# Group softmax, streamed through four buffers: smaller first and last tiles, and a drain behind each of the last waits on GpSimd

## The chip, the cores and the metric

The kernel runs on one core of a Trainium2 chip. The metric is the device time of one execution in microseconds. The kernel before was run four times: 1327.36, 1332.95, 1336.01 and 1332.74 us, median 1332.84 us. One further execution was profiled; it took 1332.72 us, and its recorded span is 1330.2 us.

## The reference

The input is a float32 tensor of 4 x 4096 x 4352. Each row of 4352 numbers is cut into 8 groups of 544, and each group gets its own softmax.

```
x_g = x.reshape(B, N, G, Dg)                      # G = 8, Dg = 544
x_g = x_g - x_g.max(axis=-1, keepdims=True)
exp = np.exp(x_g)
out = exp / exp.sum(axis=-1, keepdims=True)
return out.reshape(B, N, D).astype(np.float32)
```

Input and output are 285 MB each. There are 131,072 groups; spread over 128 partitions that is 1024 groups per partition.

## The kernel before

**Tiles.** A tile of size s holds s groups in each of the 128 partitions, so 128 x s x 544 numbers. The list `sizes` gives the tiles in order: one of 16 groups, 41 of 24 (`T`), one of 16 and one of 8; `nt` is 44 and the sum is 1024. Tile t lives in buffer t modulo 4 (`NT = 4`, each buffer as large as a tile of 24).

**Work on a tile.** ScalarE takes the exponential in place, in parts of at most 12 groups (`C`, function `parts`; line L92). The maximum is not subtracted. VectorE adds up each part (L102), takes the reciprocal of all the sums of the tile (L106), multiplies the tile by them in place (L109) and keeps a running maximum of the sums and their reciprocals (L114). At the very end `judge` tests that maximum (L119 to L134); were the test to fail, a slower and safer loop would redo everything. With this input it isn't entered.

**Queues.** SyncE's queue (SP) issues all loads in order (L139). The load of tile t waits until the store of tile t - 4 has landed, because it takes over its buffer. GpSimd's queue (POOL) issues the stores in order (L146), each when VectorE has counted the tile as scaled. The last two tiles (`LAST = 2`) are stored by SP instead (L142), behind the last load. After its last store POOL waits for the last two of its own stores (L148), drains (L149), and then waits for the two stores that SP issued; that ends the program's work.

**Loops.** ScalarE and VectorE run tile 0 by itself, then a loop of 10 turns of 4 tiles (`turns`, `looped`), then the remaining three tiles. In the loop all tiles have 24 groups. Semaphores are set back by fixed amounts after tile 0 and after each turn. The order on each engine is the order of the program text; no scheduler moves anything.

Of the kernel before, what the change touches and what calls it, by code (L numbers as in the profile page):

```python
# [9 lines left out]
def kernel(  # L10
# [5 lines left out]
    nc = tc.nc  # L16
    G = 8
    P = 128
    NT = 4
    LAST = 2  # L20
    C = 12
    LOW, HIGH = 1e-6, 1e30
    f32 = mybir.dt.float32
    X = mybir.AxisListType.X
# [6 lines left out]
    Dg = D // G  # L31
    per = N * G // P
    T = 3 * G
    sizes = [16] + [T] * (per // T - 1) + [16, 8]
    assert sum(sizes) == per
    nt = len(sizes)
    turns = (nt - 1 - LAST) // NT
    start = [sum(sizes[:t]) for t in range(nt + 1)]
    xg_all = xf.rearrange("n (g d) -> (n g) d", d=Dg)
    og_all = of.rearrange("n (g d) -> (n g) d", d=Dg)  # L40
# [5 lines left out]
    def dram(a, t):  # L46
        lo, hi = start[t] * P, start[t + 1] * P
        return a[lo:hi, :].rearrange("(p g) d -> p (g d)", p=P)

    def parts(t):  # L50
        return [(c, min(c + C, sizes[t])) for c in range(0, sizes[t], C)]

    before = [0]
    for t in range(nt):
        before.append(before[-1] + len(parts(t)))

    landed = [tc.alloc_semaphore(f"landed{b}") for b in range(NT)]
    stored = [tc.alloc_semaphore(f"stored{b}") for b in range(NT)]
    last_stored = tc.alloc_semaphore("last_stored")
    exp_done = tc.alloc_semaphore("exp_done")  # L60
    sum_done = tc.alloc_semaphore("sum_done")
    rec_done = tc.alloc_semaphore("rec_done")
    scaled = tc.alloc_semaphore("scaled")
    kept = tc.alloc_semaphore("kept")
# [18 lines left out]
    def groups(b, lo, hi):  # L83
        return bufs[b][:, lo * Dg:hi * Dg].rearrange("p (g d) -> p g d", d=Dg)

    def buf(t):
        return bufs[t % NT][:, :sizes[t] * Dg]

    def scalar_tile(t, landed_at):
        b = t % NT  # L90
        for k, (lo, hi) in enumerate(parts(t)):
            i = nc.scalar.activation(  # L92
                out=groups(b, lo, hi), in_=groups(b, lo, hi), func=Exp, scale=1.0)
            if k == 0:
                i.wait_op(landed[b], landed_at, "sem-ge")
            i.then_inc(exp_done, 1)

    def vector_tile(t, exp_at, at):
        b = t % NT
        size = sizes[t]  # L100
        for k, (lo, hi) in enumerate(parts(t)):
            i = nc.vector.reduce_sum(  # L102
                out=vals[:, b, 0, lo:hi], in_=groups(b, lo, hi), axis=X).wait_op(
                exp_done, exp_at + k + 1, "sem-ge")
        i.then_inc(sum_done, 1)
        nc.vector.reciprocal(out=vals[:, b, 1, :size], in_=vals[:, b, 0, :size]).wait_op(  # L106
            sum_done, at + 1, "sem-ge").then_inc(rec_done, 1)
        xg = groups(b, 0, size)
        nc.vector.tensor_tensor(  # L109
            out=xg, in0=xg,  # L110
            in1=vals[:, b, 1, :size].unsqueeze(2).to_broadcast([P, size, Dg]),
            op=op.mult,
        ).wait_op(rec_done, at + 1, "sem-ge").then_inc(scaled, 1)
        nc.vector.tensor_tensor(  # L114
            out=peak[:, :, :size], in0=peak[:, :, :size], in1=vals[:, b, :, :size], op=op.max,
        ).wait_op(kept, at + 1, "sem-ge").then_inc(kept, 1)
# [27 lines left out]
    for t in range(nt - LAST):  # L144
        nc.gpsimd.wait_ge(scaled, t + 1)
        nc.gpsimd.dma_start(out=dram(og_all, t), in_=buf(t)).then_inc(stored[t % NT], 16)  # L146
    for t in range(nt - NT, nt - LAST):
        nc.gpsimd.wait_ge(stored[t % NT], 16 * (t // NT + 1))  # L148
    nc.gpsimd.drain()  # L149
    nc.gpsimd.wait_ge(last_stored, 16 * LAST)  # L150

    looped = range(1, 1 + NT)
    rest = range(1 + turns * NT, nt)
    turn = before[1 + NT] - before[1]

    nc.scalar.preload_act_table(Exp)  # L156
    scalar_tile(0, 16)
    nc.scalar.sem_inc(landed[0], -16)
    with nc.scalar.Fori(0, turns):
        for t in looped:  # L160
            scalar_tile(t, 16)
# [2 lines left out]
        scalar_tile(t, 16)  # L164

    nc.vector.memset(peak[:, :, :], 0.0).then_inc(kept, 1)  # L166
    vector_tile(0, 0, 0)
    for s, n in ((exp_done, before[1]), (sum_done, 1), (rec_done, 1), (kept, 1)):
        nc.vector.sem_inc(s, -n)
    with nc.vector.Fori(0, turns):  # L170
        for k, t in enumerate(looped):
            vector_tile(t, before[t] - before[1], k)
        for s, n in ((exp_done, turn), (sum_done, NT), (rec_done, NT), (kept, NT)):
            nc.vector.sem_inc(s, -n)
    for k, t in enumerate(rest):
# [72 lines left out]
```

## Time and profile before

| what | value |
|---|---|
| median of 4 runs | 1332.84 us |
| the profiled execution, its own time | 1332.72 us |
| its span | 1330.2 us |
| VectorE busy | 1195.1 us (90%) |
| ScalarE busy | 478.4 us (36%) |
| moved by DMA | 570.45 MB, mean 429 GB/s |
| loads of 24 groups, issue to landing | 38.6 us (median of 41) |
| stores of 24 groups by GpSimd | 51.2 us (median of 41) |

The span is what the recorder covers; the 2.5 us between it and the execution's own time lie around it. "DMA share" in a table of stretches is the mean busy share of the core's 16 DMA engines; a packet is booked where it starts, so that the share of a single microsecond swings and can exceed 1. One packet here is the part of a tile that belongs to one partition, so a larger tile has longer packets.

### The profile page before, as it was taken

Reading aid. Unit: us, or ns where it says so; the run is one execution under the profiler, and the core shown is the slowest. Engines: PE = TensorE matmul, PEld = TensorE weight load, DVE = VectorE, ACT = ScalarE, POOL = GpSimd, SP = SyncE. Lnnn points to the kernel's source line nnn. Section 1 sums busy time; section 2 is a strip of 40 time slices with the busy share of each in tenths; the row PEclk is TensorE's granted clock in tenths of the full one; section 3 lists DMA queues with packets and bytes.
Section 4 is the critical chain, followed back from the end, with each engine's and each line's share of the span. In section 5 each row is a group of like instructions: output and inputs, shape, how many; then the busy total and the mean of one; then the engine's idle time right before and its main releaser. Section 6 shows DMA issues by size and latency. Waiting matters only on the chain.

```text
span 1330.2 us, 604 instructions
## 1 busy us (share of the span) xinstructions
PE 0.2 (0%) x2; PEld 0.1 (0%) x2; DVE 1195.1 (90%) x226; ACT 478.4 (36%) x88; POOL 22.7 (2%) x46
## 2 busy tenths in 40 slices
PE   0000000000000000000000000000000000000000
PEld 0000000000000000000000000000000000000000
DVE  4999999889998999999998899999999989888996
ACT  3533333344333333333344443333333333433321
POOL 0000000000000000000000000000000000000000
DMA  9999999999999999999999999999999999999997
GB/s 410 417 444 427 427 438 432 432 430 440 432 430 433 441 427 433 440 432 429 433 441 430 433 430 443 427 430 440 437 427 430 441 430 429 429 446 427 431 415 307
DMA packets 12674, 570.45 MB, mean 429 GB/s; under 512 B 1408, under 2 KB 1408, under 8 KB 1408
## 3 DMA queue, kind: packets, MB, share of 16 engines
q1 hardware_dynamic: 6624, 291.90, 50.9%
q0 software_dynamic: 6048, 278.53, 48.4%
q14 instruction: 2, 0.02, 0.0%
HBM read 285.21 MB, written 285.21 MB: 429 GB/s over the span
## 4 chain that ended last, share of the span: by engine, by line
another core or an unknown queue 71%; DVE 17%; DMA 8%; issue 2%; ACT 1%; SPq 1%; DVEq 0%; PE 0%; POOLq 0%
DVE vals L102 9%; DVE xt L109 7%; DMA xt<-in_x_dram 4%; DMA out_dram<-xt 4%; ACT xt L92 1%; SPq L139 1%; DVE vals L106 0%; DVE peak L114 0%; DVE within L124 0%; DVE extreme L120 0%; PE found L128 0%; DVE count L132 0%; DVEq L170 0%; DVE verdict L134 0%
## 5 line engine op out<-in xcount | busy, mean ns | idle before, releaser
L92 ACT ACTIVATE xt<-xt 128x6528 f32<-128x6528 f32 (+1 forms) x87 | 477.2, 5531 | 826.2 <-DMA xt<-in_x_dram 826.2
L102 DVE TENSOR_REDUCE vals<-xt 128x12 f32<-128x6528 f32 (+1 forms) x87 | 589.5, 6817 | 118.5 <-ACT xt L92 118.5
L109 DVE TENSOR_TENSOR xt<-xt,vals 128x13056 f32<-128x13056 f32 (+2 forms) x44 | 587.2, 13346 | 1.5
L146 POOL DMA_DIRECT2D out_dram<-xt x42 | 22.5, 536 | 1266.2 <-DVE xt L109 1266.2
L106 DVE RECIPROCAL vals<-vals 128x24 f32<-128x24 f32 (+2 forms) x44 | 13.1, 298 | 1.5
L114 DVE TENSOR_TENSOR peak<-peak,vals 128x48 f32<-128x48 f32 (+2 forms) x44 | 8.8, 200 | 0.0
L156 ACT ACT_TABLE_LOAD x1 | 1.3, 1283 | 0.9 <-PEq L232 0.9
L166 DVE MEMSET peak<- 128x48 f32 x1 | 0.1, 98 | 1.1 <-PEq L232 1.1
L132 DVE TENSOR_REDUCE count<-found 1x1 f32<-1x2 f32 x1 | 0.1, 149 | 0.3 <-PE found L128 0.3
L128 PE MATMUL found<-within,one 128*1 128x2 f32 x2 | 0.2, 164 | 1317.5 <-DVE within L124 1317.5
L124 DVE TENSOR_SCALAR within<-extreme 128x1 f32<-128x1 f32 x2 | 0.2, 148 | 0.0
L120 DVE TENSOR_REDUCE extreme<-peak 128x2 f32<-128x48 f32 x1 | 0.2, 203 | 0.0
L134 DVE CAST verdict<-count 1x1 int32<-1x1 f32 x1 | 0.1, 142 | 0.0
L128 PEld LDWEIGHTS found<-within,one 128*1 128x1 f32 x2 | 0.1, 80 | 1317.5 <-DVE within L124 1317.5
L232 POOL MEMSET const-float32-0.0<- 128x1 f32 x1 | 0.1, 99 | 0.3 <-issue 0.3
L232 POOL MEMSET const-bfloat16-1.0<- 128x1 bf16 x1 | 0.1, 102 | 0.0
L232 POOL MEMSET const-uint8-127<- 128x1 uint8 x1 | 0.1, 100 | 0.0
L232 POOL MEMSET const-float32-1.0<- 128x1 f32 x1 | 0.1, 99 | 0.0
L119 DVE MEMSET one<- 128x1 f32 x1 | 0.1, 59 | 0.0
## 6 DMA issues: line engine op xcount, KB each, us to landing
xt<-in_x_dram SPq DMA_DIRECT2D x41, 6528.0 KB, 38.6
out_dram<-xt POOLq DMA_DIRECT2D x41, 6528.0 KB, 51.2
xt<-in_x_dram SPq DMA_DIRECT2D x2, 4352.0 KB, 23.6
out_dram<-xt POOLq DMA_DIRECT2D x1, 4352.0 KB, 30.5
out_dram<-xt SPq DMA_DIRECT2D x1, 4352.0 KB, 16.3
xt<-in_x_dram SPq DMA_DIRECT2D x1, 2176.0 KB, 27.4
out_dram<-xt SPq DMA_DIRECT2D x1, 2176.0 KB, 11.8
```

Of the source, the lines that this page charges most:

```text
L92: i = nc.scalar.activation(out=groups(b, lo, hi), in_=groups(b, lo, hi), func=Exp, scale=1.0)
L102: i = nc.vector.reduce_sum(out=vals[:, b, 0, lo:hi], in_=groups(b, lo, hi), axis=X).wait_op(exp_done, exp_at + k + 1, "sem-ge")
L106: nc.vector.reciprocal(out=vals[:, b, 1, :size], in_=vals[:, b, 0, :size]).wait_op(sum_done, at + 1, "sem-ge").then_inc(rec_done, 1)
L109: nc.vector.tensor_tensor(out=xg, in0=xg, in1=vals[:, b, 1, :size].unsqueeze(2).to_broadcast([P, size, Dg]), op=op.mult,).wait_op(rec_done ...
L114: nc.vector.tensor_tensor(out=peak[:, :, :size], in0=peak[:, :, :size], in1=vals[:, b, :, :size], op=op.max,).wait_op(kept, at + 1, "sem-g ...
L120: nc.vector.reduce_max(out=extreme[:, :], in_=peak[:, :, :], axis=X).wait_op(kept, at + 1, "sem-ge").then_inc(tested, 1)
L124: nc.vector.tensor_scalar(out=within[:, k:k + 1], in0=extreme[:, k:k + 1], scalar1=most, scalar2=None, op0=op.is_le).then_inc(tested, 1)
L128: nc.tensor.matmul(out=found[:, :], lhsT=one[:, :], rhs=within[:, :], start=True, stop=True).then_inc(counted, 1)
L139: nc.sync.dma_start(out=buf(t), in_=dram(xg_all, t)).then_inc(landed[t % NT], 16)
L146: nc.gpsimd.dma_start(out=dram(og_all, t), in_=buf(t)).then_inc(stored[t % NT], 16)
L156: nc.scalar.preload_act_table(Exp)
L232: nc = _bacc.Bacc("TRN2", target_bir_lowering=False, num_devices=1)
```

## The change

The first tiles become 8, 12 and 12 groups in place of 16, and the last ones 16, 12 and 4 in place of 16 and 8; there are 40 tiles of 24 instead of 41, and 46 tiles in all instead of 44. Tiles that are not of 24 groups are worked on in parts of at most 8 groups (`FINE`) instead of 12. The first three tiles run ahead of the loop, whose turns remain 10. `LAST` stays 2, so SP stores the tiles of 12 and 4, and GpSimd stores the tile of 16. At the end GpSimd waits for its last eight stores, not its last two, and it drains after each of these eight waits, not once after all.

```
+    FINE = 8
+    HEAD = 3
+    TAIL = 3
...
-    sizes = [16] + [T] * (per // T - 1) + [16, 8]
+    sizes = [8, 12, 12] + [T] * (per // T - 2) + [16, 12, 4]
...
-    turns = (nt - 1 - LAST) // NT
+    turns = (nt - HEAD - TAIL) // NT
...
     def parts(t):
-        return [(c, min(c + C, sizes[t])) for c in range(0, sizes[t], C)]
+        size = C if sizes[t] == T else FINE
+        return [(c, min(c + size, sizes[t])) for c in range(0, sizes[t], size)]
...
-    for t in range(nt - NT, nt - LAST):
+    for t in range(nt - LAST - 8, nt - LAST):
         nc.gpsimd.wait_ge(stored[t % NT], 16 * (t // NT + 1))
-    nc.gpsimd.drain()
+        nc.gpsimd.drain()
     nc.gpsimd.wait_ge(last_stored, 16 * LAST)
...
-    looped = range(1, 1 + NT)
-    rest = range(1 + turns * NT, nt)
-    turn = before[1 + NT] - before[1]
+    looped = range(HEAD, HEAD + NT)
+    rest = range(HEAD + turns * NT, nt)
+    turn = before[HEAD + NT] - before[HEAD]
...
-    scalar_tile(0, 16)
-    nc.scalar.sem_inc(landed[0], -16)
+    for t in range(HEAD):
+        scalar_tile(t, 16)
+        nc.scalar.sem_inc(landed[t % NT], -16)
...
-    vector_tile(0, 0, 0)
-    for s, n in ((exp_done, before[1]), (sum_done, 1), (rec_done, 1), (kept, 1)):
+    for t in range(HEAD):
+        vector_tile(t, before[t], t)
+    for s, n in ((exp_done, before[HEAD]), (sum_done, HEAD), (rec_done, HEAD), (kept, HEAD)):
         nc.vector.sem_inc(s, -n)
```

More of the change, by code (lines that the diff above doesn't have):

```diff
@@ L171 @@
         for k, t in enumerate(looped):
-            vector_tile(t, before[t] - before[1], k)
+            vector_tile(t, before[t] - before[HEAD], k)
         for s, n in ((exp_done, turn), (sum_done, NT), (rec_done, NT), (kept, NT)):
```

## The prediction, made before the changed kernel was run

> **What bounds the kernel now.** I first read the page, then its DMA part against the engines' busy times.
>
> ```profile
> span 1330.2 us, 604 instructions
> ...
> PE 0.2 (0%) x2; PEld 0.1 (0%) x2; DVE 1195.1 (90%) x226; ACT 478.4 (36%) x88; POOL 22.7 (2%) x46
> ...
> DMA packets 12674, 570.45 MB, mean 429 GB/s; under 512 B 1408, under 2 KB 1408, under 8 KB 1408
> ...
> q1 hardware_dynamic: 6624, 291.90, 50.9%
> q0 software_dynamic: 6048, 278.53, 48.4%
> ```
>
> The two queues' packets fill 99.3% of the 16 DMA engines' span; VectorE, the next, has 90%. Where the missing part lies, a table of stretches shows (columns: stretch and length, then busy time of PE, PEld, DVE, ACT and POOL, clock, DMA share, GB/s).
>
> ```profile
> 0.00:2.00 2.00, 0.00 (x0) 0.00 (x0) 0.10 (x1) 1.08 (x1) 0.20 (x4) 1.00 0.35 87
> 2.00:34.00 32.00, 0.00 (x0) 0.00 (x0) 14.29 (x4) 12.34 (x4) 0.00 (x0) 1.00 0.99 421
> 240.00:1240.00 1000.00, 0.00 (x0) 0.00 (x0) 902.35 (x162) 358.96 (x65) 17.06 (x32) 1.00 1.00 433
> 1290.00:1305.00 15.00, 0.00 (x0) 0.00 (x0) 14.93 (x4) 3.27 (x1) 0.00 (x0) 1.00 0.91 392
> 1305.00:1308.00 3.00, 0.00 (x0) 0.00 (x0) 3.00 (x3) 0.56 (x1) 0.00 (x0) 1.00 0.08 35
> 1308.00:1324.00 16.00, 0.19 (x2) 0.09 (x2) 9.63 (x10) 0.00 (x0) 0.00 (x0) 1.00 0.98 418
> 1324.00:1328.00 4.00, 0.00 (x0) 0.00 (x0) 0.00 (x0) 0.00 (x0) 0.00 (x0) 1.00 0.07 28
> ```
>
> At 433 GB/s the bytes need 1317.4 us, so 12.8 us of span are not full transfer. The stretches shown account for 12.0 of them: 1.3 us at the start, 0.3 to 34, 1.4 in 1290 to 1305, 2.8 in the hole from 1305 to 1308, 0.3 to 1324, 3.7 to 1328, 2.2 after it. Now the point on which I decide: in the hole the share is 0.08 and in 1324 to 1328 it is 0.07, close to one engine of 16 (0.0625). I read this as one slow engine, about 4.5 us behind the other 15, which works through the hole on its backlog and sets the last landing at 1328.7. Fifteen engines waste the hole; the one that ends the program doesn't.
>
> The tail of the timeline, the issues and the drain (a row of GpSimd's queue that the page doesn't count as busy):
>
> ```profile
> 1288.42 9.27 DVE L102 TENSOR_REDUCE vals<-xt 128x12 f32<-128x6528 f32 x2
> 1298.01 9.22 DVE L109 TENSOR_TENSOR xt<-xt,vals 128x8704 f32<-128x8704 f32 x1
> 1307.27 10.01 SPq L142 DMA_DIRECT2D out_dram<-xt  x2
> 1312.21 4.69 DVE L109 TENSOR_TENSOR xt<-xt,vals 128x4352 f32<-128x4352 f32 x1
> ```
> ```profile
> xt<-in_x_dram SPq DMA_DIRECT2D x1, 2176.0 KB, 27.4
> out_dram<-xt SPq DMA_DIRECT2D x1, 4352.0 KB, 16.3
> out_dram<-xt SPq DMA_DIRECT2D x1, 2176.0 KB, 11.8
> ```
> ```profile
> L149 POOLq DRAIN  x1: 3496/3496/3496, 1314.6 to 1314.6; - x1
> ```
>
> The last store is issued at 1316.9 and lands 11.8 us later though its bytes need 5.1 us.
>
> **The change part by part.** A group costs 0.643 us each way (278.5 kB at 433 GB/s), 1.287 us both ways.
>
> *Head.* Before, the first four loads hold 88 groups, 56.6 us of transfer. After, they hold 56, 36.0 us, until about 38. Is a store there by then? The first load landed 13.0 us after issue; 8 groups fewer take 5.1 off, so it lands at 8.8. ScalarE 3.8 (the 8-group form), VectorE 4.7 + 0.2 + 4.7, with gaps and 0.3 on POOL: the first store goes out at about 22.7 instead of 38.8. Tile 1 takes VectorE 4.7 + 2.4 + 0.2 + 6.9 + 0.2 (half the 13.76 us multiply of 24 groups), so its store goes out near 37; tile 2's near 51.5. Load 4 waits for store 0. While store 0 is on its way the engines have it to move, and all that is queued, loads 36.0 and store 0 5.1, ends at about 43; store 1 has then been waiting since 37 and covers load 4's issue. If store 0 took the 30.5 us that the first one took before, it would land at 53; work of loads, store 0 and store 1 lasts to 51 and store 2 goes out at 51.5, a hole of 2 us at most. I take 0, by the share of 0.99 to 1.00 near it; ends 0 and +2. VectorE begins 5.1 us earlier, which is worth nothing while DMA is full.
>
> *Two more tiles,* so four more DMAs. All 88 of them together cannot have cost the slow engine more than its 4.5 us of lag, 0.05 each: 0 to +0.2 us, I take 0.1. The Trainium skill, "DMA: Bandwidth & Descriptors", section on the anatomy of one DMA, speaks against the change here: about 2.0 us fixed per DMA beside its bytes. Four of these on the path would make, as an estimate, 8 us and about 1340.7 us; this trace, full at 433 GB/s through 1000 us, shows that cost covered by other queued transfers.
>
> *Middle.* Tiles of 24, loop and their waits are as before: 0. The smaller parts (at most 8 groups) touch head and tail alone; ScalarE has 64% of its time free, and VectorE pays 0.1 us for 2 x 4.68 instead of 9.27 on the tile of 16.
>
> *Tail.* The last tile of 24 was there at 1254.8 with 24 groups behind it; now 32 are behind it, 8 x 1.287 = 10.3 us earlier: 1244.5. Then ScalarE's first part 5.65, VectorE 28.0 (1260.44 to 1288.42 now) to 1278.1, the 16 groups 18.9 to 1297.0, the 12 groups 14.5 (4.68 + 2.41 + 0.2 + 6.9 + 0.2, gaps) to 1311.5, the 4 groups 5.1 (2.41 + 0.2 + 2.35 + gaps) to 1316.6. So the last tile is scaled as late as before (1316.9), but what then is left is smaller: 2.6 us of bytes instead of 5.1. The slow engine needs it by 1328.4 - 2.6 - 1.0 for issue = 1324.8: 8.2 us of slack, and it never runs dry. The loads may run up to 7.7 us later against the stores than they do now (the last load of 24 landed 7.7 us after the issue of the next, 1247.0). And the last load may be as slow as the 27.4 us row: that one was issued at 1274.3 with 72 groups of stores and 8 of loads behind it, this one will have 56 and 4, 20 x 0.643 us fewer, so it is issued at 1287.2, lands at 1314.6 and is scaled, after ScalarE's 2.0 and VectorE's 5.1, at 1321.7. Each alone still makes the 1324.8. Gain: 0, because the bytes of the slow engine are the same. Ends: 0, and +4 if both delays add up.
>
> *Waits and drains.* Behind them on POOL stands only the wait for SP's stores; nobody waits for POOL until the end. One drain is 3.5 us (L149), others of POOL at the program's end 0.03 to 0.11. The store of 16 groups goes out at 1297.3; eight drains of 3.5 are 28 us, to 1325.3. The last also follows that store's landing: by the last store of POOL before (25.9 us) at 1323.2, plus 3.5 = 1326.7, under the 1328.7 of SP's last store. By the 30.5 us row it would be 1331.3. I take 0, two microseconds from being exposed; ends 0 and +2.6.
>
> *Sum.* 1330.2 + 0 + 0.1 + 0 + 0 = 1330.3 of span, and 2.5 around it: 1332.8; the profiled execution stands 0.1 us under the median of the runs. With the drain so close I say 1333.0.
>
> **Rivals.** *Faster:* the chain of waits names ScalarE and VectorE in the tail, and if these and not the slow engine set the end, the first landing is 5.1 us earlier and the last store 2.6 us shorter: 1332.7 - 7.7 = 1325.0. For it speaks the hole at 1305. Against it: the engine at work in the hole, and a DMA share of 1.00 that cannot pass on an early start.
>
> *Slower:* drains that cannot start while a store of POOL is under way. Then all eight follow the landing at 1323.2, 28 us to 1351.2, 22.5 later than now: 1355. It decides from eight drains longer than 0.7 us each on. For it: the one drain took 3.5 us with nothing left in its queue, thirty times the others. Against it: the others show that a drain with no work is short.
>
> *A late tail:* the last load lands after about 1318 and the slow engine runs dry: +4, 1337.
>
> *No change:* that is my forecast.
>
> **How the numbers follow.** No change 0.62; faster 0.15; serial drains 0.13; late tail 0.10. About 0.5% (6.7 us) can be told from no change by a measurement of this kernel. Half the late tail lies beyond it with the spread of the runs, and a little of the forecast on the fast side: faster 0.17, same 0.63, slower 0.20. The forecast's own range is the spread of the runs, 1328 to 1338. For 8 in 10 it takes in the faster case (1325) and the late tail with that spread (1341), not the serial drains.
>
> **What would show it.** Right: full DMA share from 34 to 1290, first store near 22.7, the last VectorE multiply ending near 1316, one engine alone in the last 4 us, the last drain ended before the last landing. Wrong: a share under 0.9 between 38 and 55; a hole after the last load without one busy engine; a drain as the last thing before the end; or a last landing several microseconds before 1328, which would show that the slow engine was no floor.

## The result, and the profile after

The changed kernel is slower by a third of a per cent: the ratio of its time to that of before is 1.0034, with a 95% interval of 1.0022 to 1.0045, which is 4.5 us of 1327.6 (2.9 to 6.0). The medians are 1334.06 us (52 runs, 1326.63 to 1339.07) and 1327.62 us (78 runs of the kernel before, 1324.52 to 1337.06). Single executions of either kernel spread over 12 us, and unevenly: 40 of the 78 of before lie under 1328 us, 2 of the 52 of the change. So the medians are 6.4 us apart, the means (1333.84 and 1329.36) 4.5 us, as the ratio says. The profiled execution of the changed kernel took 1335.07 us with a span of 1333.2 us, against 1332.72 and 1330.2 of the one profile of before that the prediction had. That one profile was of an execution 5.1 us above the median that 78 runs gave later. So the two profiles differ by 3.0 us in span, less than the kernels do, and the place where time went is read from the stretches, not from that difference.

The middle is as forecast. From the page of the changed kernel, its head line and its DMA issues (size, then median time from issue to landing), and one row of its timeline (start, duration, engine, line):

```profile
span 1333.2 us, 628 instructions
...
xt<-in_x_dram SPq DMA_DIRECT2D x40, 6528.0 KB, 46.9
out_dram<-xt POOLq DMA_DIRECT2D x40, 6528.0 KB, 42.9
```
```profile
23.66 0.67 POOL L150 DMA_DIRECT2D out_dram<-xt  x1 [23.20 <-DVE xt L113]
```

The first store goes out at 23.7 instead of 38.8 us. But look at the two medians. Before, a load of 24 groups took 38.6 us from issue to landing and a store 51.2; now they take 46.9 and 42.9. The sum is the same (89.8 us both times). By the median the loads of the long middle have become 8.3 us slower and the stores 8.3 us faster, though no tile there differs. Below I call the *gap* the time by which a load lands after the next load has been issued. A tile's transfers come every 30.9 us, so the gap is the load's time less 30.9: 7.7 us before, 16.0 now.

Next the stretches of the changed kernel (columns as in the prediction: stretch, length, busy PE, PEld, DVE, ACT, POOL, clock, DMA share, GB/s), and the tail of its timeline:

```profile
240.00:1240.00 1000.00, 0.00 (x0) 0.00 (x0) 903.14 (x162) 357.64 (x64) 17.00 (x32) 1.00 1.00 433
1240.00:1281.00 41.00, 0.00 (x0) 0.00 (x0) 37.95 (x8) 14.85 (x3) 0.53 (x1) 1.00 0.98 422
1281.00:1287.00 6.00, 0.00 (x0) 0.00 (x0) 6.00 (x3) 3.88 (x2) 0.53 (x1) 1.00 0.53 226
1287.00:1316.00 29.00, 0.00 (x0) 0.00 (x0) 28.86 (x9) 7.22 (x3) 0.53 (x1) 1.00 0.96 401
1316.00:1319.00 3.00, 0.00 (x0) 0.00 (x0) 3.00 (x3) 0.53 (x1) 0.00 (x0) 1.00 0.14 58
1319.00:1330.00 11.00, 0.19 (x2) 0.09 (x2) 5.17 (x10) 0.00 (x0) 0.00 (x0) 1.00 0.96 407
1330.00:1332.00 2.00, 0.00 (x0) 0.00 (x0) 0.00 (x0) 0.00 (x0) 0.00 (x0) 1.00 0.02 9
```
```profile
1251.60 11.18 ACT L96 ACTIVATE xt<-xt 128x6528 f32<-128x6528 f32 x2 [19.80 <-DMA xt<-in_x_dram]
...
1285.51 0.53 POOL L150 DMA_DIRECT2D out_dram<-xt  x1 [30.44 <-DVE xt L113]
...
1304.36 0.53 POOL L150 DMA_DIRECT2D out_dram<-xt  x1 [18.32 <-DVE xt L113]
...
1318.37 5.44 SPq L146 DMA_DIRECT2D out_dram<-xt  x2
...
1321.02 2.42 DVE L113 TENSOR_TENSOR xt<-xt,vals 128x2176 f32<-128x2176 f32 x1
```

There are two holes in the DMA share: 6 us at 0.53, which end when VectorE has finished the last tile of 24 and POOL issues its store (1285.5), and 3 us at 0.14, which end when SP issues the store of the tile of 12 (1318.4). In both VectorE is busy without a break. And the last tile of 24 was there at 1251.6, not at 1244.5. At the end no single engine is left over: the share goes from 0.96 to 0.02, and by the trace's landing records the 16 engines finish within 1.2 us of each other (1330.0 to 1331.2). In the profile of before, one engine landed 3.3 us after the other 15.

The landing records show one thing more. Each transfer lands in 16 parts, one from each engine. In this execution of the changed kernel the parts of one load of 24 lie within 2.4 us at 76 us, and the spread grows steadily, to 15.8 us at 1221 us. The engines drift apart. In the execution of before that was profiled it stays under 6.5 us for the loads and grows to 13.3 us for the stores.

### The profile page after: what moved, and what is told of

Same layout as the page of the kernel before. It is cut to its first block, busy times and chain, and to the rows that moved or that the text cites. A ratio compares the mean times of both kernels' runs of the same rounds, so it can differ in the third digit from the quotient of the medians.

```text
span 1333.2 us, 628 instructions
## 1 busy us (share of the span) xinstructions
PE 0.2 (0%) x2; PEld 0.1 (0%) x2; DVE 1196.5 (90%) x235; ACT 478.9 (36%) x91; POOL 23.7 (2%) x48
## 4 chain that ended last, share of the span: by engine, by line
DMA 68%; DVE 26%; ACT 5%; issue 1%; PE 0%; DVEq 0%; POOLq 0%; SPq 0%
DMA xt<-in_x_dram 36%; DMA out_dram<-xt 32%; DVE vals L106 13%; DVE xt L113 12%; ACT xt L96 5%; DVE vals L110 0%; DVE peak L118 0%; DVE within L128 0%; DVE extreme L124 0%; PE found L132 0%; DVE count L136 0%; DVE verdict L138 0%; DVEq L176 0%; DVEq L180 0%; SPq L249 0%
## 5 line engine op out<-in xcount | busy, mean ns | idle before, releaser
L96 ACT ACTIVATE xt<-xt 128x6528 f32<-128x6528 f32 (+2 forms) x90 | 477.7, 5353 | 836.7 <-DMA xt<-in_x_dram 836.7
L106 DVE TENSOR_REDUCE vals<-xt 128x12 f32<-128x6528 f32 (+2 forms) x90 | 589.9, 6595 | 123.5 <-ACT xt L96 123.5
L113 DVE TENSOR_TENSOR xt<-xt,vals 128x13056 f32<-128x13056 f32 (+4 forms) x46 | 587.5, 12772 | 1.6
L110 DVE RECIPROCAL vals<-vals 128x24 f32<-128x24 f32 (+4 forms) x46 | 13.4, 292 | 1.6
L118 DVE TENSOR_TENSOR peak<-peak,vals 128x48 f32<-128x48 f32 (+4 forms) x46 | 9.1, 198 | 0.0
## 6 DMA issues: line engine op xcount, KB each, us to landing
xt<-in_x_dram SPq DMA_DIRECT2D x40, 6528.0 KB, 46.9
out_dram<-xt POOLq DMA_DIRECT2D x40, 6528.0 KB, 42.9
out_dram<-xt SPq DMA_DIRECT2D x1, 3264.0 KB, 10.3
```

Of the source, the lines that this page charges most:

```text
L96: i = nc.scalar.activation(out=groups(b, lo, hi), in_=groups(b, lo, hi), func=Exp, scale=1.0)
L106: i = nc.vector.reduce_sum(out=vals[:, b, 0, lo:hi], in_=groups(b, lo, hi), axis=X).wait_op(exp_done, exp_at + k + 1, "sem-ge")
L113: nc.vector.tensor_tensor(out=xg, in0=xg, in1=vals[:, b, 1, :size].unsqueeze(2).to_broadcast([P, size, Dg]), op=op.mult,).wait_op(rec_done ...
L118: nc.vector.tensor_tensor(out=peak[:, :, :size], in0=peak[:, :, :size], in1=vals[:, b, :, :size], op=op.max,).wait_op(kept, at + 1, "sem-g ...
```

## The experiments

*Lateness theory:* VectorE enters the tail late, by the gap that the head sets, and the DMA engines run dry. *Tile-count theory:* more and smaller tiles cost, wherever they are. *Drain theory:* the eight drains cost. All ratios are to the kernel before, in the experiments run on the same chip (the record names no chip for the row of the change); the load column is the median from issue to landing of a load of 24 in that kernel's profile.

| kernel | first tiles | last tiles | load, us | ratio (95% interval) |
|---|---|---|---|---|
| before, repeated | 16 | 16, 8 | 38.8 | 1.0007 (0.9987 to 1.0028) |
| drains alone | 16 | 16, 8 | 36.6 | 1.0010 (0.9990 to 1.0030) |
| small last tiles | 16 | 12, 8, 4 | 37.8 | 1.0012 (0.9987 to 1.0037) |
| before, ScalarE sums | 16 | 16, 8 | 36.7 | 1.0008 (0.9988 to 1.0027) |
| before, VectorE 7 us late | 16 | 16, 8 | 36.5 | 1.0041 (1.0024 to 1.0059) |
| the change | 8, 12, 12 | 16, 12, 4 | 46.9 | 1.0034 (1.0022 to 1.0045) |
| its tail back | 8, 12, 12 | 16, 8, 8 | 48.3 | 1.0043 (1.0016 to 1.0071) |
| its head to 16s | 16, 16 | 16, 12, 4 | 42.4 | 1.0045 (1.0023 to 1.0067) |
| small head, old tail | 8, 8 | 16, 8 | 38.1 | 1.0027 (1.0005 to 1.0050) |
| head of one 8 | 8 | 16, 12, 4 | 38.6 | 1.0061 (1.0037 to 1.0086) |
| the change, ScalarE sums 3 tiles | 8, 12, 12 | 16, 12, 4 | 48.2 | 1.0014 (0.9995 to 1.0033) |
| the change, ScalarE sums 7 tiles | 8, 12, 12 | 16, 12, 4 | 48.2 | 1.0023 (1.0004 to 1.0042) |
| head of one 8, ScalarE sums | 8 | 16, 12, 4 | 38.6 | 1.0072 (1.0058 to 1.0087) |

**The kernel before, once more.**

> The kernel before, unchanged, for a second profile of it and for what a comparison of equal kernels shows. All theories: ratio 1.000 within 0.002; the loads again land some 4 to 8 us after the issue of the next load, and the DMA engines run dry once in the tail, near 1305.

Equal kernels gave 1.0007, so ratios below 1.002 tell nothing by themselves here. The profile is of the longest of the 12 executions, 1335.8 us, as long as the profiled one of the changed kernel. Here the parts of a store of 24 land up to 17.2 us apart, the last tile of 24 is there at 1257.0 us instead of 1254.7, and the DMA share is 0.29 from 1306 to 1311, about the time when SP issues the store of 16 (1309.5). So a late last tile and a hole in the tail come without the change too.

**The drains alone.**

```
-    for t in range(nt - NT, nt - LAST):
+    for t in range(nt - LAST - 8, nt - LAST):
         nc.gpsimd.wait_ge(stored[t % NT], 16 * (t // NT + 1))
-    nc.gpsimd.drain()
+        nc.gpsimd.drain()
```

> The kernel before with one thing of the change alone: eight waits with a drain behind each at the end of GpSimd's queue. Phase theory and tail theory: no difference beyond 1 us, since GpSimd's last wait is for SP's stores, which land later. Drain theory: 4 to 5 us slower than before, with a drain as the last thing ahead of the end.

No difference: 1.0010. The drains of this kernel and of the changed one, as rows of GpSimd's queue (minimum, median and maximum in ns, then first and last start):

```profile
L149 POOLq DRAIN  x8: 34/34/27722, 1284.9 to 1313.2; - x8
```
```profile
L153 POOLq DRAIN  x8: 34/34/18404, 1304.3 to 1323.3; - x8
```

One drain is long and the other seven take 34 ns. The long one is the first; it starts as soon as POOL has issued its last store (1304.36 in the changed kernel) and ends at 1322.75, 1.8 us after that store's landing at 1320.9; in the kernel with the drains alone it ends at 1312.7, 1.8 us after the landing at 1310.9. The last landing of all is 1331.2 and 1325.0, so GpSimd waits for SP's stores in both. Drain theory falls: the drains are not what the end waits for.

**One half undone at a time.**

```
-    HEAD = 3
+    HEAD = 2
...
-    sizes = [8, 12, 12] + [T] * (per // T - 2) + [16, 12, 4]
+    sizes = [16, 16] + [T] * (per // T - 2) + [16, 12, 4]
```

> The changed kernel with two first tiles of 16 in place of 8, 12 and 12; its last tiles (16, 12, 4) and its eight waits and drains stay. Phase theory (the small first tiles put every later load some 8 us later against the stores, so that VectorE enters the tail 7 us late and the DMA engines run dry twice there): the last load of 24 groups lands about 8 us after the issue of the load that follows it, instead of 15.7 us; the last tile is scaled near 1317 instead of 1323.4; time as before within 1 us. Tail theory (last tiles of 16, 12 and 4 are dearer by themselves, whatever the head): still 4 to 5 us slower than before. Drain theory (the eight drains cost): still slower.

```
-    sizes = [8, 12, 12] + [T] * (per // T - 2) + [16, 12, 4]
+    sizes = [8, 12, 12] + [T] * (per // T - 2) + [16, 8, 8]
```

> The changed kernel with its first tiles (8, 12, 12) and drains, but last tiles 16, 8 and 8 in place of 16, 12 and 4. Phase theory: the gap from the issue of a load to the landing of the one before it stays near 16 us, VectorE's tail is 28.0 + 18.9 + 9.9 + 9.9 us behind a late last load of 24, holes in the DMA share stay; 3 to 5 us slower than before. Tail theory: the tail is that of before with one more tile of 8, so at least half of the loss is gone: 0 to 2 us slower than before. Drain theory: 4 to 5 us slower.

Both were as slow as the whole change, as far as the intervals tell (1.0045 and 1.0043). For the second that is what lateness theory said. For the first it was a miss: two first tiles of 16 don't bring the gap of before back. A load takes 42.4 us, a gap of 11.6:

```profile
xt<-in_x_dram SPq DMA_DIRECT2D x40, 6528.0 KB, 42.4
out_dram<-xt POOLq DMA_DIRECT2D x40, 6528.0 KB, 46.9
```

That profile can't show where the time went: it is of the shortest of the 11 executions (1328.2 us), and in it VectorE scaled the last tile by 1314.9, earlier than in the profile of before (1316.9).

**Head and tail apart.** The next kernels keep 41 tiles of 24, so that one end can be that of before. Each is the changed kernel with one list replaced, and `HEAD` to match (and `TAIL = 4` in the third):

```
+    sizes = [8, 8] + [T] * (per // T - 1) + [16, 8]
```

> Two first tiles of 8 ahead of 41 tiles of 24 and the last tiles of before (16 and 8), 45 tiles; the waits and drains of the change. Gap means: how long after the issue of a load the load ahead of it lands (before 4 to 8 us, changed kernel 15.6). Lateness theory (the time lost is DMA idle in the tail because VectorE comes late to the last tiles, and it comes late by the gap): a gap of up to 8 us gives the time of before within 1 us, one of 11 us or more gives 2 to 5 us slower with a hole in the DMA share ahead of the store of 16 or 8. Tile-count theory (each kernel with more and smaller tiles pays, wherever they are): 4 to 5 us slower at any gap, without holes in the tail.

```
+    sizes = [16] + [T] * (per // T - 1) + [12, 8, 4]
```

> The first tile of before (16), 41 tiles of 24, and last tiles of 12, 8 and 4 in place of 16 and 8; 45 tiles; the waits and drains of the change. Lateness theory: gap 4 to 8 us as before, VectorE needs 28.0 + 14.5 + 9.9 + 5.1 = 57.5 us from the last tile of 24 on instead of 56.7, so the last tile is scaled within 1 us of before and the time is that of before within 1 us. Tile-count theory: 4 to 5 us slower.

```
+    sizes = [8] + [T] * (per // T - 1) + [16, 12, 4]
```

> One first tile of 8, 41 tiles of 24, and the last tiles of the change (16, 12, 4); 45 tiles; its waits and drains. Lateness theory: with a gap of up to 8 us the last tile is scaled near 1317 and the time is within 2 us of before; with a gap of 11 us or more it is scaled 4 to 8 us later and the time is 2 to 5 us longer, as with the two kernels that undid one half. Tile-count theory: 4 to 5 us slower at any gap.

Three small last tiles behind the head of before cost nothing that can be told (1.0012). That speaks against tile-count theory, for the head of one 8 has as many tiles and costs 1.0061; it doesn't exclude the 1.003 to 1.004 of that theory, since the interval reaches 1.0037. Two first tiles of 8 ahead of the tail of before are enough for 1.0027; the loads near its end land 10 us after the next issue, between the two cases that the expectation named, and its profile has a hole of 4 us at a share of 0.18 ahead of the store of 16. The head of one 8 was a clear miss for lateness theory: its gap is 7.7 us like that of before, and it is the slowest of the three, 8 us. The hole of the first of these two, and two stretches of the second:

```profile
1303.00:1307.00 4.00, 0.00 (x0) 0.00 (x0) 4.00 (x3) 2.02 (x1) 0.00 (x0) 1.00 0.18 78
```
```profile
1313.00:1318.00 5.00, 0.00 (x0) 0.00 (x0) 4.45 (x3) 2.02 (x1) 0.00 (x0) 1.00 0.44 185
...
1328.00:1333.00 5.00, 0.00 (x0) 0.00 (x0) 0.00 (x0) 0.00 (x0) 0.00 (x0) 1.00 0.05 19
```

After a hole, a share of 0.05, one engine of 16 for most of the time, fills the last microseconds. The landing records show where it fell behind: of the second tile of 24 to be stored, 15 engines had landed their part by 114.8 us and the last one by 124.6.

**VectorE's lateness, added and taken away.** To the kernel before, one useless sum is added ahead of the last tile of 16:

```
     for k, t in enumerate(rest):
+        if k == 1:
+            nc.vector.reduce_sum(
+                out=extra[:, :], in_=groups(rest[1] % NT, 0, C), axis=X).wait_op(
+                exp_done, before[t] - before[rest[0]] + 1, "sem-ge")
         vector_tile(t, before[t] - before[rest[0]], k)
```

> The kernel before with its head, tiles and waits, and one extra sum over 12 groups (6.95 us, into a scratch tile that nothing reads) on VectorE just ahead of the last tile of 16. This makes VectorE late by 7 us in the tail and changes nothing else. Lateness theory: the last two tiles are scaled 7 us later, a hole of DMA share of up to 7 us opens ahead of their stores, and the kernel is 3 to 6.5 us slower than before, about as much as the change. If lateness of VectorE in the tail costs nothing because one slow DMA engine sets the end: 0 to 1 us slower.

It costs 0.41%, 5.4 us (3.2 to 7.8), for 6.95 us of lateness. Timeline rows and stretches of its profile:

```profile
1284.57 6.95 DVE L178 TENSOR_REDUCE extra<-xt 128x12 f32<-128x6528 f32 x1
...
1310.28 10.01 SPq L143 DMA_DIRECT2D out_dram<-xt  x2
```
```profile
1303.00:1312.00 9.00, 0.00 (x0) 0.00 (x0) 9.00 (x3) 0.00 (x0) 0.00 (x0) 1.00 0.21 91
...
1325.00:1328.00 3.00, 0.00 (x0) 0.00 (x0) 0.00 (x0) 0.00 (x0) 0.00 (x0) 1.00 0.46 191
```

A hole of 9 us at 0.21 ends with the store of 16. No engine is left alone at the end (the last store's 16 parts land from 1327.0 to 1328.4): I read this as a slow engine's backlog that is used up within such a hole, so that from there on VectorE's delay moves the end.

The other direction: ScalarE forms the sums of the last tiles itself, one group per instruction, and VectorE only multiplies.

```
+            i = nc.scalar.activation(
+                out=groups(b, g, g + 1)[:, 0, :], in_=groups(b, g, g + 1)[:, 0, :], func=Exp,
+                scale=1.0, accum_out=tails[:, b, 0, g:g + 1])
...
-        vector_tile(t, before[t] - before[rest[0]], k)
+        vector_tail(t, k)
```

> The changed kernel, with the sums of its last three tiles (16, 12, 4) formed by ScalarE along with the exponential, group by group, so that VectorE only multiplies them. Nothing else differs: head, gap and number of tiles are those of the change. Lateness theory: gap still near 15.6 us, the tile of 16 is scaled some 9 us earlier (near 1295), the hole ahead of the store of 12 is gone or under 1 us; at least half of the loss is back, 0 to 2.5 us slower than before. Tile-count theory: still 4 to 5 us slower than before.

> The changed kernel with the sums of its last seven tiles (four of 24, then 16, 12 and 4) formed by ScalarE. Head, gap and tiles are those of the change. Lateness theory: no hole is left between 1240 us and the last store, the time is that of before within 1.5 us. Tile-count theory, or a cost of the head by itself: 3 to 5 us slower than before.

> The kernel before, with the sums of its last three tiles (24, 16, 8) formed by ScalarE, and the waits and drains of the change. VectorE is then early in the tail. Lateness theory: the kernel before has next to no such hole in its shorter executions, so at most 1 us is won; were the tail of before late as well, 2 to 4 us would be won.

> The kernel with one first tile of 8 and last tiles of 16, 12 and 4, which was 8 us slower than before, now with the sums of its last four tiles (24, 16, 12, 4) formed by ScalarE. Lateness theory: at least half of the 8 us is back, 0 to 4 us slower than before. If its loss is that of a DMA engine that falls behind early in the run (its stores landed 10 us after those of the other 15 engines by 125 us): still 6 to 9 us slower.

In the first of these the store of 16 goes out at 1289.7 instead of 1304.4, and the holes are closed:

```profile
1243.82 11.18 ACT L98 ACTIVATE xt<-xt 128x6528 f32<-128x6528 f32 x2 [19.63 <-DMA xt<-in_x_dram]
...
1289.70 0.53 POOL L177 DMA_DIRECT2D out_dram<-xt  x1 [11.43 <-DVE xt L140]
```
```profile
1281.00:1287.00 6.00, 0.00 (x0) 0.00 (x0) 6.00 (x1) 0.00 (x0) 0.00 (x0) 1.00 0.94 405
1287.00:1316.00 29.00, 0.19 (x2) 0.09 (x2) 13.18 (x14) 10.44 (x32) 0.53 (x1) 1.00 1.00 433
1316.00:1319.00 3.00, 0.00 (x0) 0.00 (x0) 0.00 (x0) 0.00 (x0) 0.00 (x0) 1.00 0.93 395
```

But not all of this is the edit's doing. The last tile of 24, which the edit doesn't touch, is there at 1243.8, 7.8 us earlier than in the changed kernel's profile and close to the 1244.5 of the prediction, and that makes 7.8 of the 14.7 us. Head and middle are those of the change, and the gap is even longer (48.2 - 30.9 = 17.3 us). What differs is that in this execution, of 1326.6 us, the engines stay together: the parts of every load of 24 land within 2.5 us. So the lateness of the last tile of 24 in the changed kernel's profile came with the drift of its engines in that execution; the gap alone doesn't make it.

The ratio is 1.0014, and with seven tiles treated so 1.0023. Both are nearer to 1 than the change's 1.0034, but their intervals overlap with its: the times alone don't show how much comes back, and the second one's interval still excludes 1. Its 3.0 us are a miss for lateness theory, which allowed 1.5, and lie where a cost of the head by itself was expected. The kernel before gains nothing by the same edit (1.0008), so no version here beats it. And the head of one 8 stays where it was (1.0072): its loss isn't VectorE's lateness. In its profile the same early event is seen again, 15 engines by 112.6 us and the last by 126.8.

**What follows.** The four kernels that keep the first tile of 16, and leave VectorE in time, lie between 1.0007 and 1.0012. All eight with another head lie between 1.0014 (the only one whose interval holds 1) and 1.0072, whatever their last tiles. This points to the first tiles, 1300 us before the place where the loss shows; the small last tiles cost nothing that can be told.

How the head costs time is not shown as a whole. Three pieces are. First, VectorE's lateness in the tail costs: 6.95 us of it cost 5.4 us (3.2 to 7.8). Second, the head moves the loads back. In two profiles whose engines stay together, that of the change with ScalarE's sums of three tiles and that of the kernel before with the same edit, the last tile of 24 is there at 1243.8 and 1247.8 us. The first has 8 groups more behind it, which is worth 10.3 us, so it is 6.3 us late. Whether these 6.3 us alone open a hole isn't shown, for in both ScalarE's sums make VectorE early. Third, where the engines drift apart that tile comes later still, by 7.8 us in the profile of the change, and by 9.2 us in the longest profiled execution of the kernel before (1257.0 against 1247.8). So the holes in the one profile of the change are head and drift together. The head of one 8 shows a drift that begins early: one engine falls back within 127 us and ends alone. Whether the change's head makes drift more frequent, which would fit its few short executions, is open, and so is what makes the engines drift.

## Why the prediction was right, and where it was not

The time lay in the range, and a change below what it called tellable was its likeliest case. The change that it forecast was not right: nothing, where 4.5 us were lost (2.9 to 6.0). That 1333.0 came within 1.1 us of the measured median is luck, two errors that cancel: it began from an execution 5.1 us above the median of 78 runs, and it added 0.3 us where the medians differ by 6.4. Of the signs that it named, one of "wrong" came, a hole after the last load without a busy engine (a share of 0.14 from 1316 to 1319, 0.00 in the last of these three), and two of "right" didn't: the last multiply of VectorE ended at 1323.4, not near 1316, and no engine was alone in the last 4 us.

- *The bound.* Right: a DMA share of 1.00 at 433 GB/s over the thousand microseconds of the middle, in both kernels.
- *The slow engine as the floor.* Right for both profiles of before, where one engine lands 3.3 and 4.4 us after the other 15, wrong as a floor for the profiled execution of the change: there all 16 engines finish within 1.2 us. I read this as the two holes having used up the lag.
- *Head.* The first store was put at 22.7 and came at 23.7, and no hole opened near 50. As a count of idle time in the head "I take 0" was right; as all that the head costs it is the step that failed: the kernel with the added sum aside, those that lost are the ones with another head than 16. The prediction asked only whether DMA would idle in the head; it had no term for the order in which loads and stores alternate from there on. The gap went from 7.7 to 16.0 us, which by the two profiles without drift puts the last tile of 24 back by 6.3 us. How much of the 4.5 us that makes is open.
- *Tail.* VectorE's durations were right: from the last tile of 24 to the last scaled tile 72.1 us were summed, 71.8 came (1251.6 to 1323.4). The start was late by 7.1 us, inside the "up to 7.7" that the text allowed; in the execution without drift it came at 1243.8. What it got wrong is the deadline. It was worked out for the last store alone, when only 4 groups are left to move. When the store of 12 is issued 16 groups are left, and it was due, by the same rule, at 1328.4 - 16 x 0.643 - 1.0 = 1317.1; it went out at 1318.4. That makes 1.3 us. For the first hole, 6 us at a share of 0.53, the text had no term, for it follows one slow engine alone. The 16 parts of the load of 12, the last transfer issued by then, landed from 1280.8 to 1298.4: the engines that were ahead had nothing to do until POOL issued the next store at 1285.5.
- *Two more tiles.* Right as far as it can be told: one tile more at the end costs 1.0012 (0.9987 to 1.0037). The Trainium skill ("DMA: Bandwidth & Descriptors", anatomy of one DMA) has a fixed cost of about 2 us per DMA, on GpSimd's path; for the two DMAs more of that kernel this would be, as an estimate, 4 us. Measured are 1.6 us, with an interval from -1.7 to 4.9, which holds both that and nothing.
- *Waits and drains.* Right in price. The premise of the slower rival held, a drain does wait for POOL's stores, but the seven behind it cost 34 ns each and not 3.5 us.
- *The rivals.* The late tail had the right size, +4 us at a chance of 0.10, but not for its reason: its last load was to land after about 1318, and in the profile it landed at 1314.5. The faster one failed as argued: VectorE's early start passed nothing on.

## What to carry to other kernels

Where DMA is full from end to end, an early start is worth nothing, but the sizes of the first tiles can still cost time 1300 us later. The two medians of issue to landing show how loads and stores interleave, but they don't clear a head: with two first tiles of 8, and with one, the load's median stayed at 38 us, and both kernels lost. For the tail, work out a deadline for every store from the bytes that still have to move, not for the last store alone. And take several runs before a time is built on one profiled execution, and compare profiles of executions of about the same length: here one kernel's executions differ by more than the kernels do.

## What the runs showed of the hardware

- The gap between loads and stores tends to stay at certain values. Where single landings are followed, it is 3.9, later 7.7 us in the kernel before, 11.6 with two first tiles of 16 and 15.4 to 17.0 in the changed kernel. 2, 4, 6 and 8 times 1.93 us are 3.9, 7.7, 11.6 and 15.4, and 1.93 us is what the trace gives for one packet of a tile of 24 (52,224 bytes). The Trainium skill, "DMA: Bandwidth & Descriptors", section on queues, rings and completion order, says that an engine goes round its queues packet by packet; these values fit that, if its packet, typically some 9 to 17 descriptors, is the one of the profile, which no run here shows. Other profiles fit less well: the gap rose from 4 to 10 us with two first tiles of 8, and was 17 to 20 with the tail back at 16, 8 and 8.
- The 16 engines drift apart in some executions and not in others, with the same tiles in the middle. The parts of a load of 24 land within 2.5 us to the end in one (the change with ScalarE's sums of three tiles, 1326.6 us), and up to 15.8 us apart in another (the change, 1335.1 us).
- A GpSimd drain issued while its stores are under way lasts until 1.8 us after the last of them has landed; issued after the landing it takes 3.5 us; a further drain takes 34 ns.
- A lone tile of 8 ahead of tiles of 24 leaves one DMA engine 10 to 14 us behind the others by 127 us, in both kernels that had it, and their shortest times, 1334.0 and 1331.6 us, lie above the medians of before on the same chips (1326.1 and 1325.7). The cause wasn't looked for.
